# One layer of a hybrid encoder: TensorE's instructions kept in the order of the kernel's text, the other engines ordered by a timeline model

## The chip, the cores and the metric

The kernel runs on one NeuronCore of a Trainium2 chip. The core has five engines with an instruction stream each: TensorE (PE in the profile, its weight loads PEld), VectorE (DVE), ScalarE (ACT), GpSimd (POOL) and SyncE (SP, whose stream issues most of the DMAs; SPq is its queue). Each engine works through its own stream in order; an instruction that needs another engine's result waits at its place, and what stands behind it in the same stream waits too. The metric is the time of one execution on the device in microseconds (us), lower is better.

## The reference

A sequence of 2048 positions of width 1024, in float32, goes through one layer. Cut to what matters:

```python
h = rmsnorm(x, norm_mix_w)
proj = h @ w_in                       # 1024 -> 5648 columns
u_b, u_c, u_h, z, xbc, dt_raw = split(proj)
y_a = u_b * conv3(u_c * u_h)          # short gated convolution
xs, B, C = split(silu(conv4(xbc)))
dt = softplus(dt_raw + dt_bias)       # 16 heads
y_b = ssd_scan(xs, dt, -exp(a_log), B, C) + d_skip * xs
y_b = grouped_rmsnorm(y_b * silu(z))
x = x + concat(y_a, y_b) @ w_out
h = rmsnorm(x, norm_mlp_w)
x = x + square(relu(h @ w_up)) @ w_down   # 1024 -> 4096 -> 1024
return rmsnorm(x, final_norm_w)
```

The scan is chunked: inside a chunk the running sum of `dt * a` gives decay factors exp(difference of two running sums); between chunks a state per head is carried on.

## The kernel before

**The products.** Positions lie in four blocks of 512 (two make a half), features on the 128 partitions. A float32 operand is split in two: a part rounded to fp32r by ScalarE (`whi` L100 for weights, `uh` L205 or L347 for activations), and the rest, by a subtraction on VectorE (`wlo` L101, `ul` L206 or L348). A float32 product is then three fp32r matmuls with 128x128 weights and 512 columns: high by high, high by low, low by high (L113 to L115, L276 to L278). The large projections combine their blocks into seven products in place of eight (the names b11, t1, t2, b21, t3, b22, t4 stand for them), so VectorE also makes sums of weights and activations, and adds products (L730, L874, L1018) when it takes them out of PSUM.

**The stages**, in the order of the text of `trunk`: `start` (RMSNorm of the first two blocks: square and sum into `facc` L489/L492, the column sums `pst` L132, the root `rs` L144, its spread over partitions `prb` L178, the scaling L501; then the gate's first columns and the part for dt); `first_half` (the in-projection of half 0, with VectorE and ScalarE normalising half 1 beside it, L371 to L380); `second_half` (of half 1, with the scan of half 0 beside it); the out-projection with the scan of half 1 beside it; the MLP up and down; the last RMSNorm.

**The dt part** (`dt_part`, L616 to L676), once for each of the four blocks: a sum of products `pd` on TensorE (L625), a copy by ScalarE (L629), four small transposes `pt` on TensorE (L633), the softplus as a chain of small VectorE operations on 128x64 (L635 to L656, with one Exp on ScalarE, L644, in it), the running sums `pc` on TensorE (L662, L663), a copy (L664), a transpose `pr` on TensorE (L671), and the stores to `dt_d` and `rd_d` from which the scan loads. It is a generator, and its caller draws it on between pieces of other work:

```python
nc.vector.tensor_tensor(                                  # L656, end of the softplus
    out=three(e), in0=three(v), in1=self.a_neg..., op=ALU.mult)
yield
yield
pc = psum("tp", "pc", 2)
nc.tensor.matmul(pc[:, 0:64], tri, e, start=True, stop=True)   # L662
```

and in `start`, for each of the two first blocks, after the block's z columns (`group`, L534):

```python
for _ in dts:
    next(work, None)      # work: normalising, or sums of activations; no matmuls
```

**The scan** (`Scan`, L1181) handles 32 pieces (a chunk of one of two head groups), half of them beside `second_half` and half beside the out-projection. A piece has its loads (`load`, L1205: `xd` L1220, `bc`, `dec`, all from DRAM, on SP's queue), a front (L1245: transposes `ptx` L1253 and `ptb` L1255 and the product L1256 on TensorE; then on ScalarE the copies `xtok` and `btok`, eight Relu activations `dec` L1267 and one Exp L1268) and a back (L1278: `yo` L1287, `st` L1289, `yd` L1292 on TensorE, the state's update L1302/L1303 on VectorE, the norm's `pss` L1317). Both are generators; `after` in `second_half` and `hook` in `unit` (L1464) draw one step between products, so the text itself lays the scan's small matmuls between the large ones.

**What sets the order.** All of `trunk` is written inside a tile context. The program's text gives each engine a list of instructions in text order; when the context closes, a scheduler sets the order in which each engine's stream holds them, by a model of how long each takes and what it waits for. Dependencies become semaphore waits. In the kernel before this is done with the context's defaults for all engines, with no order written out by hand: TensorE's stream departs from the text at 47 places (an instruction that stands behind one with a later place in the text), 809 of its 11,514 instructions stand somewhere else than in the text, by up to 95 places forwards and 48 back. The dt part's small matmuls and the scan's transposes are among them.

## Time and profile before

| | us |
|---|---|
| median of 3 timed runs | 2664.36 (2661.9 to 2666.43) |
| the profiled execution | 2658.11 |
| its span in the trace | 2656.4 |
| TensorE busy | 2602.2 (98%), 12,024 matmuls |
| VectorE busy | 1874.3 (71%) |
| ScalarE busy | 1436.5 (54%) |
| GpSimd busy | 146.1 (6%) |
| DMA | 536.96 MB, the one queue q1 60.9% of 16 engines' span |
| mean granted TensorE clock | 0.995 |

The span runs from the first to the last record of the trace; the profiled execution's own time is 1.7 us longer, and 6.25 us under the median of the timed runs. A group's row reads: line, engine, operation, output tile and input tiles, shapes, count; then the busy time of all of them, the mean of one, and the idle time just before them with what ended most of it. A row of the timeline reads: start, duration, engine, line, operation, and in square brackets the engine's idle time before it and whose work released it.

### The profile page before, as it was taken

The numbers are of one execution on the slowest core, as the hardware profiler recorded it, in microseconds if no ns is written. First come the engines' busy times: TensorE is split into PE (matmuls) and PEld (weight loads), VectorE is DVE, ScalarE is ACT, GpSimd is POOL, SyncE is SP. The second block draws the span as 40 slices with busy tenths as digits, with TensorE's granted clock in tenths as the row PEclk, the third lists the DMA queues.
The fourth block names the chain that finished last, engine by engine and source line by source line (L and its number), as shares of the span: only waits on it lengthen the run. The fifth ranks groups of instructions, "written<-read, shape, count | busy, mean of one in ns | idle before, by whom it ended". The sixth has DMA issues, their size and how long they took to land.

```text
span 2656.4 us, 33528 instructions
## 1 busy us (share of the span) xinstructions
PE 2602.2 (98%) x12024; PEld 2124.8 (80%) x12024; DVE 1874.3 (71%) x2524; ACT 1436.5 (54%) x2178; POOL 146.1 (6%) x162
## 2 busy tenths in 40 slices
PE   7999999999999999998999999999999999999998
PEld 5788888778877888776888888888887888888887
DVE  7977867667667666666678675744447877888985
ACT  6654345766567566857336555755555434444443
POOL 0010000111111001111000000000000000000001
PEclk9999999999999999999999999999999999999999
DMA  3545735555555578867566786765558554665762
GB/s 145 196 174 182 278 143 202 182 152 174 169 161 168 165 262 267 254 200 232 193 208 214 258 315 254 258 234 178 209 183 297 155 152 153 206 219 165 249 209 71
DMA packets 292871, 536.96 MB, mean 202 GB/s; under 512 B 26208, under 2 KB 141920, under 8 KB 292704
## 3 DMA queue, kind: packets, MB, share of 16 engines
q1 hardware_dynamic: 292704, 534.82, 60.9%
q8 instruction: 94, 1.54, 0.2%
q14 instruction: 73, 0.60, 0.1%
HBM read 354.89 MB, written 179.83 MB: 201 GB/s over the span
## 4 chain that ended last, share of the span: by engine, by line
PE 59%; issue 26%; ACT 5%; DMA 4%; DVE 4%; POOL 1%; SPq 0%; POOLq 0%; DVEq 0%; ACTq 0%
PE px L276 9%; PE px L277 9%; PE px L278 9%; PE py L276 4%; PE py L277 4%; PE py L278 4%; PE pm L113 4%; PE pm L114 4%; PE pm L115 3%; PE pw L276 2%; PE pw L277 2%; PE pw L278 2%; ACT whi L100 1%; ACT dec L1267 1%; DMA dec<-rd_d 1%
## 5 line engine op out<-in xcount | busy, mean ns | idle before, releaser
L276 PE MATMUL px<-uh,whi 128*128 128x512 f32 x1672 | 657.7, 393 | 6.8 <-DVE acc L1018 1.8
L278 PE MATMUL px<-uh,wlo 128*128 128x512 f32 x1672 | 652.2, 390 | 0.0
L277 PE MATMUL px<-ul,whi 128*128 128x512 f32 x1672 | 651.9, 390 | 0.0
L276 PEld LDWEIGHTS px<-uh,whi 128*128 128x128 f32 x1672 | 314.5, 188 | 82.2 <-DVE acc L1018 3.2
L101 DVE TENSOR_TENSOR wlo<-wraw,whi 128x1024 fp32r<-128x1024 f32 x214 | 223.2, 1043 | 222.2 <-ACT whi L100 216.4
L278 PEld LDWEIGHTS px<-uh,wlo 128*128 128x128 f32 x1672 | 314.4, 188 | 66.4 <-issue 0.2
L277 PEld LDWEIGHTS px<-ul,whi 128*128 128x128 f32 x1672 | 314.6, 188 | 63.5
L100 ACT CAST whi<-wraw 128x1024 fp32r<-128x1024 f32 x214 | 193.6, 905 | 302.5 <-PE px L277 223.4
L276 PE MATMUL py<-uh,whi 128*128 128x512 f32 x836 | 327.4, 392 | 4.4 <-DVE acc L1018 3.4
L100 ACT CAST whi<-s 128x1024 fp32r<-128x1024 f32 x210 | 219.7, 1046 | 206.8 <-PE py L277 81.8
L277 PE MATMUL py<-ul,whi 128*128 128x512 f32 x836 | 325.6, 389 | 0.0
L278 PE MATMUL py<-uh,wlo 128*128 128x512 f32 x836 | 325.4, 389 | 0.0
L101 DVE TENSOR_TENSOR wlo<-s,whi 128x1024 fp32r<-128x1024 f32 x210 | 255.2, 1216 | 79.9 <-ACT whi L100 78.1
L113 PE MATMUL pm<-uh,whi 128*128 128x512 f32 (+1 forms) x648 | 253.1, 392 | 2.1 <-ACT uh L205 2.1
L114 PE MATMUL pm<-ul,whi 128*128 128x512 f32 (+1 forms) x648 | 249.9, 386 | 0.0
L115 PE MATMUL pm<-uh,wlo 128*128 128x512 f32 (+1 forms) x648 | 249.5, 385 | 0.0
L276 PEld LDWEIGHTS py<-uh,whi 128*128 128x128 f32 x836 | 156.9, 188 | 39.8 <-DVE acc L1018 3.8
L278 PEld LDWEIGHTS py<-uh,wlo 128*128 128x128 f32 x836 | 156.9, 188 | 33.0 <-DVE wlo L101 0.2
L277 PEld LDWEIGHTS py<-ul,whi 128*128 128x128 f32 x836 | 157.0, 188 | 32.0
L276 PE MATMUL pw<-uh,whi 128*128 128x512 f32 x418 | 163.5, 391 | 0.7 <-ACT pw L283 0.7
L347 ACT CAST uh<-rh 128x1024 fp32r<-128x1024 f32 (+1 forms) x128 | 120.3, 943 | 80.4 <-PE py L278 62.4
L278 PE MATMUL pw<-uh,wlo 128*128 128x512 f32 x418 | 162.9, 390 | 0.0
(232 smaller groups left out, 3763.2 us busy)
## 6 DMA issues: line engine op xcount, KB each, us to landing
hid_d<-e SPq DMA_DIRECT2D x96, 512.0 KB, 3.9
rh<-hid_d SPq DMA_DIRECT2D x96, 512.0 KB, 4.4
wraw<-w_in SPq DMA_DIRECT2D x68, 512.0 KB, 3.9
wraw<-w_down SPq DMA_DIRECT2D x104, 256.0 KB, 3.7
wraw<-w_up SPq DMA_DIRECT2D x48, 512.0 KB, 4.5
dec<-rd_d SPq DMA_DIRECT2D x32, 512.0 KB, 5.8
wraw<-w_out SPq DMA_DIRECT2D x32, 512.0 KB, 5.1
x_d<-xt SPq DMA_DIRECT2D x64, 256.0 KB, 3.2
```

The lines of the kernel that those rows point to most:

```text
L100: nc.scalar.copy(hi, raw)
L101: eng.tensor_tensor(out=lo, in0=raw, in1=hi.bitcast(F32), op=ALU.subtract)
L113: nc.tensor.matmul(out, whi, hi, start=(k == 0), stop=False)
L114: nc.tensor.matmul(out, whi, lo, start=False, stop=False)
L115: nc.tensor.matmul(out, wlo, hi, start=False, stop=(k == nk - 1))
L276: nc.tensor.matmul(p, hi, h[0], start=not seeded and k == 0, stop=False, **kw)
L277: nc.tensor.matmul(p, hi, h[1], start=False, stop=False, **kw)
L278: nc.tensor.matmul(p, lo, h[0], start=False, stop=(k == len(g) - 1), **kw)
L347: nc.scalar.copy(p[i][0], t)
L1267: nc.scalar.activation(dec[:, i], dec[:, i], AF.Relu, bias=t["a"][:, i : i + 1], scale=-1.0)
```

## The change

Two arguments of the tile context. The first has the scheduler use its timeline model of the engines and queues in place of the simpler one. The second puts the whole of `trunk` in a scope in which TensorE's instructions aren't moved: its stream is the text's order. The other engines are ordered by the scheduler as before, now with the other model.

```diff
-    with tile.TileContext(nc) as tc:
-        trunk(tc, *args, out)
+    with tile.TileContext(nc, schedule_with_timeline_sim=True) as tc:
+        with tc.manual_schedule(engines={mybir.EngineType.PE}):
+            trunk(tc, *args, out)
```

The instructions and their number stay the same on TensorE, VectorE and SyncE; ScalarE has three loads of its function table fewer. TensorE now departs from the text nowhere. On VectorE 1,397 of some 2,500 instructions stand elsewhere than before (by up to 53 places), on ScalarE 946 of some 2,180 (up to 30), on SyncE 813 of some 1,500 (up to 61). Three places follow; names carry the number of the buffer (it differs from one build to the other), and "x4" is four such rows in a run.

TensorE in `start`, the running sums of block 0's dt part (`pc`, `pr`), before: they stand between matmuls of the z columns (`pm`), 84 instructions further behind the `pt` transposes than in the text.

```order
L113 MATMUL pm<-uh_461,whi 128x512
L114 MATMUL pm<-ul_462,whi 128x512
L115 MATMUL pm<-uh_461,wlo 128x512
L113 MATMUL pm<-uh_469,whi 128x512
L662 MATMUL pc<-dts,tri 128x64
L663 MATMUL pc<-dts,ones_r 128x64
L114 MATMUL pm<-ul_470,whi 128x512
L115 MATMUL pm<-uh_469,wlo 128x512
L113 MATMUL pm<-uh_477,whi 128x512
L671 MATMUL pr<-ident,dts 64x128
L625 MATMUL pd<-uh_409,wdt 32x512
```

The same place now:

```order
L625 MATMUL pd<-uh_296,wdt 32x512
L625 MATMUL pd<-ul_297,wdt 32x512
L633 MATMUL pt<-ident,dts 128x32 x4
L662 MATMUL pc<-dts,tri 128x64
L663 MATMUL pc<-dts,ones_r 128x64
L671 MATMUL pr<-ident,dts 64x128
L113 MATMUL pm<-uh_411,whi 128x512
L114 MATMUL pm<-ul_412,whi 128x512
```

`pt`, `pc` and `pr` now follow one another, with none of the z columns' matmuls between them: those that stood there are ahead of the `pd` products or behind `pr`. Block 1 and the two blocks of half 1 have the same four groups in the text, in `start` side by side as here.

VectorE over the same stretch, the end of block 0's softplus and what follows it, before:

```order
L653 SCALAR_TENSOR_TENSOR dts<-dts 128x64
L206 TENSOR_TENSOR ul_290<-x_183,uh_289 128x512
L655 SCALAR_TENSOR_TENSOR dts<-dts 128x64
L520 TENSOR_TENSOR x_183<-x_218,x_183 128x512
L656 TENSOR_TENSOR dts<-dts,hb 128x64
L206 TENSOR_TENSOR ul_462<-x_216,uh_461 128x512
L664 COPY dts<-pc 128x128
L206 TENSOR_TENSOR ul_470<-x_216,uh_469 128x512
L666 TENSOR_TENSOR dts<-dts 128x64
L672 COPY dts<-pr 64x128
```

and now:

```order
L377 TENSOR_TENSOR facc<-lx 128x512
L650 TENSOR_SCALAR dts<-dts 128x64
L652 SCALAR_TENSOR_TENSOR dts<-dts 128x64 x6
L380 TENSOR_TENSOR facc<-facc,lx 128x512
L652 SCALAR_TENSOR_TENSOR dts<-dts 128x64
L380 TENSOR_TENSOR facc<-facc,lx 128x512
L653 SCALAR_TENSOR_TENSOR dts<-dts 128x64
L655 SCALAR_TENSOR_TENSOR dts<-dts 128x64
L656 TENSOR_TENSOR dts<-dts,hb 128x64
L380 TENSOR_TENSOR facc<-facc,lx 128x512 x2
L664 COPY dts<-pc 128x128
```

The small steps of the softplus stand among the sums of squares of the next half (`facc` from `lx`, a tile loaded from DRAM), in place of the low parts `ul` and the sums of activations.

TensorE in `second_half`, the opening of the scan of half 0 (`ptx`, `ptb`), before:

```order
L276 MATMUL py<-uh_3713,whi 128x512
L277 MATMUL py<-ul_3714,whi 128x512
L278 MATMUL py<-uh_3713,wlo 128x512
L276 MATMUL py<-uh_3717,whi 128x512
L1287 MATMUL yo<-bc,state_3777 128x128 x3
L1253 MATMUL ptx<-ident,xd 128x128 x4
L1255 MATMUL ptb<-ident,bc 128x128
L1256 MATMUL ptb<-bc 128x128
L1287 MATMUL yo<-bc,state_3777 128x128
L277 MATMUL py<-ul_3718,whi 128x512
```

and now:

```order
L276 MATMUL py<-uh_3605,whi 128x512
L277 MATMUL py<-ul_3606,whi 128x512
L278 MATMUL py<-uh_3605,wlo 128x512
L1253 MATMUL ptx<-ident,xd 128x128 x4
L1255 MATMUL ptb<-ident,bc 128x128
L1256 MATMUL ptb<-bc 128x128
L276 MATMUL px<-uh_3655,whi 128x512
L277 MATMUL px<-ul_3656,whi 128x512
L278 MATMUL px<-uh_3655,wlo 128x512
```

The transposes stand 43 instructions earlier in the stream, after the product of the step before, where the text draws the scan's first front. (The `yo` products moved behind them, to the text's place.)

## The prediction

> **What bounds the kernel now.** I read the busy shares, then the waits of TensorE, then its busy time by stretches.
>
> ```profile
> PE 2602.2 (98%) x12024; PEld 2124.8 (80%) x12024; DVE 1874.3 (71%) x2524; ACT 1436.5 (54%) x2178; POOL 146.1 (6%) x162
> ...
> PE pst L132 <- DVE facc L492: 12.7, 1, 12.7
> ...
> 0.00:100.00 100.00, 83.66 (x362) 1.00 0.46 165
> 235.00:450.00 215.00, 215.00 (x949) 1.00 0.58 208
> 545.00:970.00 425.00, 422.18 (x2088) 1.00 0.55 171
> ```
>
> (Waits: us in total, times, longest. Stretches: window, length, PE busy and matmuls, clock, DMA share, GB/s.) TensorE is busy for 98% of the span. Its idle time is 2656.4 - 2602.2 = 54 us, of which 16.3 lie in the first 100 us, 12.7 of those at the very first product, before there is anything else to do. In the steady stretch a matmul costs 215/949 = 0.2265 us. So TensorE is the bound, and there are 41 us at most that a better order could win from behind the start's first wait. On the other side every microsecond that TensorE newly waits lengthens the run, since nothing later has slack to give it back.
>
> The method follows from this. TensorE's text order is known. For each place of it I took the time at which TensorE gets there before (that of the matmul standing behind that place) and the time at which the operands are ready before. Where ready is later than arrival, TensorE will now stand; it used to fill this time with matmuls that the text has later. Then I shift by what the other engines' new order puts ahead of the producer. Most of the stream comes out ready in time; the terms below are the places that don't.
>
> A wait also costs clock. After 2.92 us of idling the matmuls start 0.43 us apart:
>
> ```profile
> 1219.30 0.33 PE L1255 MATMUL ptb<-ident,bc 128*128 128x128 f32 x1 [2.92 <-DVE state L1303]
> ...
> 1219.94 0.63 PE L114 MATMUL pm<-ul,whi 128*128 128x512 f32 x1
> 1220.37 0.63 PE L115 MATMUL pm<-uh,wlo 128*128 128x512 f32 x1
> ...
> 1223.33 0.40 PE L113 MATMUL pm<-uh,whi 128*128 128x512 f32 x1
> ```
>
> From 1219.94 to 1223.33 are 8 matmuls: 3.39 us instead of 8 x 0.2265 = 1.8, so 1.6 us on top of a wait of this length.
>
> **Term 1, the first normalisation: +6.** The first low part `ul` (L206) stands ahead of the scalings before; now the order of VectorE puts seven more scalings (L501) and four sums (L489/L492) ahead of it.
>
> ```profile
> 19.96 0.69 DVE L206 TENSOR_TENSOR ul<-x,uh 128x512 fp32r<-128x512 f32 x1
> 20.56 2.07 DVE L501 SCALAR_TENSOR_TENSOR x<-x,cv,facc 128x512 f32<-128x512 f32 x3
> 28.48 1.28 ACT L461 ACT_TABLE_LOAD   x1
> 29.77 0.22 ACT L461 ACTIVATE hb<-hb 128x16 f32<-128x16 f32 x1
> 33.98 3.08 DVE L492 TENSOR_TENSOR facc<-facc,sq 128x512 f32<-128x512 f32 x4
> ```
>
> 7 x 0.69 + 4 x 0.77 = 7.9 us later for the first L114. The Exp of `hb` (L461) with its table load now stands ahead of the root on ScalarE, 1.28 + 0.22 = 1.5 more. The scalings have to be done anyway, and TensorE runs through the rest of the first columns faster once they are; I give back 3.4 and take 6, bounds 0 (all swallowed by the later products) and 9.4. The Trainium skill ("ScalarE: Activation LUTs", What ACT_TABLE_LOAD costs) adds a drain of some 1.38 us to each load, 2.66 in all. In the trace the load at 28.48 lasts 1.28 and the Exp starts at 29.77, right behind it, so the row shows no drain; by the page term 1 would be 1.4 more.
>
> **Term 2, the dt part of blocks 0 and 1: +44.** This is the largest piece. In the text the running sums `pc` stand directly behind `pt` and `pr` directly behind `pc`; the softplus chain on VectorE lies between `pt` and `pc`.
>
> ```profile
> 50.26 0.43 PE L633 MATMUL pt<-ident,dts 32*128 32x32 f32 x4
> 69.79 0.33 PE L662 MATMUL pc<-dts,tri 128*128 128x64 f32 x2
> 70.93 0.27 PE L671 MATMUL pr<-ident,dts 128*64 128x128 f32 x1
> ...
> 75.99 0.43 PE L633 MATMUL pt<-ident,dts 32*128 32x32 f32 x4
> 97.66 0.33 PE L662 MATMUL pc<-dts,tri 128*128 128x64 f32 x2
> ...
> 494.09 0.28 DVE L635 TENSOR_REDUCE dts<-pt 128x64 f32<-128x128 f32 x1
> 503.71 0.41 PE L662 MATMUL pc<-dts,tri 128*128 128x64 f32 x2 [0.57 <-DVE dts L656]
> ```
>
> Before, TensorE did matmuls of the z columns from 50.6 to 69.8; now they stand behind `pr`, or are already done. Block 0: `pc` starts 69.79 - 50.26 = 19.5 after `pt`, `pr` another 1.1 later, 20.6 together. VectorE has 12 operations of 128x512 more ahead of L656 (8.2 us at 0.69), among them the sums from `lx`, which comes by DMA; against that it gets rid of some of the operations that stood between the steps of the chain. I take 26. Block 1: from the end of `pt` (75.99 + 0.4) to 97.66 are 21.3; nothing is added ahead in the new order, and about 5 are saved since VectorE has run ahead during the first wait: 16, with 1.6 for the clock 18. Sum 44. The lower bound is the chain with VectorE free for it, which half 1 shows: 494.09 to 503.71, 9.6 each, 19 for both. The upper one is 20.6 + 8.2 + 21.3 + 1.1 + 2 x 1.6 and 3 for a late `lx` (a load of `xd` takes 3.1 to land, below), 57.
>
> **Term 3, the opening of each scan: +18.** `ptx` is now reached where the text has it:
>
> ```profile
> 467.03 0.39 PE L276 MATMUL px<-uh,whi 128*128 128x512 f32 x1
> 472.11 0.33 SPq L309 DMA_DIRECT2D a<-w_in  x1
> 473.91 0.43 SPq L1220 DMA_DIRECT2D xd<-xs_d  x1
> DMA to landing us min/median/max: 3.1/3.1/3.1
> 477.99 0.60 PE L1253 MATMUL ptx<-ident,xd 128*128 128x128 f32 x4
> 480.46 2.45 ACT L1267 ACTIVATE dec<-dec,dd 128x128 f32<-128x128 f32 x8 [0.53 <-DMA bc<-xs_d]
> ...
> 973.99 0.39 PE L113 MATMUL pm<-uh,whi 128*128 128x512 f32 x1
> 976.55 0.43 SPq L1220 DMA_DIRECT2D xd<-xs_d  x1
> 982.23 0.60 PE L1253 MATMUL ptx<-ident,xd 128*128 128x128 f32 x4
> ```
>
> `xd` lands 3.1 us after its issue, at 477.0, 9.9 after TensorE's arrival. SP's queue now has the weight load L309 behind the scan's loads, and this load waited for VectorE until 472.11, so `xd` goes out up to 3 us earlier: 9.9 - 3 + 1.6 = 8.5 (bounds 4 and 11.5). The second scan: 982.23 - 973.99 = 8.2 late, and I find nothing that brings the load forward: 8.2 + 1.6 = 9.8 (bounds 5 and 11).
>
> **Term 4, the dt part of half 1: +16.** Here the text has other matmuls between the groups, so only the rest is exposed (the first `pc` is in term 2's rows).
>
> ```profile
> 499.35 0.39 PE L276 MATMUL pw<-uh,whi 128*128 128x512 f32 x1
> 523.77 0.39 PE L276 MATMUL py<-uh,whi 128*128 128x512 f32 x1
> 533.01 0.41 PE L662 MATMUL pc<-dts,tri 128*128 128x64 f32 x2 [1.60 <-DVE dts L656]
> ```
>
> Arrival 499.35, start 503.71, 0.57 of it idle already: 3.8; the copy of `pd` on ScalarE (L629) now stands behind the eight Relus (2.45 us, term 3's row) and their Exp, which takes about as long, 4.9 against a slack of about 2: 2.9 more, 6.7. The second: 9.2 - 1.6 + 1.6 for the clock = 9.2. Bounds together 8 and 20.
>
> **Term 5, later places: +26.5.**
>
> ```profile
> 226.06 3.35 DVE L172 RECIPROCAL facc<-facc 128x512 f32<-128x512 f32 x1
> ...
> 1235.18 0.39 PE L113 MATMUL pm<-uh,whi 128*128 128x512 f32 x1
> ...
> 1243.42 0.80 PE L1317 MATMUL pss<-ssq,ones_r 128*128 128x128 f32 x2 [5.37 <-DVE facc L1492]
> ...
> 2023.32 0.39 PE L276 MATMUL px<-uh,whi 128*128 128x512 f32 x1
> 2034.05 0.50 PE L276 MATMUL py<-uh,whi 128*128 128x512 f32 x1 [3.38 <-DVE acc L1018]
> 2035.68 0.79 PE L276 MATMUL px<-uh,whi 128*128 128x512 f32 x1 [0.43 <-DVE acc L1018]
> ...
> 2621.44 0.28 PE L113 MATMUL pm<-uh,whi 128*128 128x256 f32 x1
> ```
>
> `pss` at 1235.18: 8.2 late, 5.4 idle already, and a square behind eight Relus: 4. The down projection: the accumulation read at 2035.6 is wanted at 2023.3, 12.3 late, less the 3.8 idle in the rows there, and the product before it is late too, which I count for 2.5: 6. The last norm (from 2621.44): 3. Seven places with 0.4 to 3.8 us late, such as those behind the reciprocal of 3.35 us: 5.5 in all (estimate). The rest of the scan: TensorE isn't moved, but ScalarE's order puts the next piece's Relus, which wait for a load, ahead of copies that TensorE waits for: +8, taken near the lower end of -10 to +45 (no row before shows it; the stretch from 545 to 970 had only 2.8 us of idling, and each of 32 pieces would lose at most the Relus' 2.45 less what lies open).
>
> **The sum:** 6 + 44 + 18 + 16 + 26.5 = 110.5. On the profiled execution's 2658.1 this is 2768.6; the median of the runs shown lies 6.25 above that execution, so 2775.
>
> **Rivals.** *Chains alone:* the timeline model brings the producers forward where it sees TensorE stand. For it: VectorE is busy for 71% only, SP's load moved aside. Against: in the new order VectorE's big operations stand among the small ones of block 0. Term 2 falls to 19, term 3 to 9, term 4 to 8: 42 less, 2733. *Relus first:* ScalarE's order costs each of 32 scan pieces 1.4 us more than the 8 of term 5: +45, 2820. For it: the order of ScalarE does put them first; against: ScalarE is 54% busy and the pieces are some 13 us apart ((970 - 545)/32). *The other side:* in text order TensorE loses only the two chains of 9.5 us, or even less if the model puts them ahead of everything, while the timeline order removes the stalls that stand now: at most the 41 us found above, since the first 12.7 remain. If it removed all and lost 22 it would be 2645; it decides if terms 2 to 4 stay under the waits won. The rows of term 2 speak against it: nothing stands between `pt`, `pc` and `pr`. *It does nothing:* only 47 departures in 11,514 instructions; but the dt part is among them.
>
> **How the numbers follow.** Forecast (2775) 0.60, chains alone (2733) 0.17, Relus first (2820) 0.17, the other side (2645) 0.04, nothing (within 0.2% of 2664, about what a measurement here can tell) 0.02. The terms' bounds make 2775 uncertain by about 30 either way (they don't all go to one end); reaching down past 2733 and up past 2820 leaves about 2 in 10: 2720 to 2826. Slower 0.60 + 0.17 + 0.17 = 0.94, same 0.02, faster 0.04.
>
> **What would show it.** Right: TensorE's waits list `pc` L662 for VectorE's L656 with over 10 us each in the first 130 us, `ptx` for the load of `xd` at both openings with 5 to 9, and its busy time is near 2602 plus some 10 for slow clock; and it is busy for some 35 to 45 of the first 100 us, not 83.66. Wrong: `pc` waits of 9 or less (term 2 is the chain alone); idling spread over the scan's stretches (545 to 970 and 1000 to 1234) of more than 10 us (Relus first); or a wait at `pc` that is hidden, with the stalls listed at the top gone (the other side).

## The result and the profile after

The changed kernel takes 2855.8 us (median of 4 runs, 2846.9 to 2862.8) where the kernel before takes 2664.0 beside it: a ratio of 1.072 (95% interval 1.069 to 1.075), 192 us more. The prediction said slower, 2775 us, 2720 to 2826. The direction was right, the size was not: 110 us had been forecast, and the time lies above the range.

The page of the changed kernel, span and busy shares:

```profile
span 2850.8 us, 33696 instructions
...
PE 2643.6 (93%) x12024; PEld 2148.9 (75%) x12024; DVE 1884.2 (66%) x2524; ACT 1434.3 (50%) x2175; POOL 146.8 (5%) x162
```

TensorE does the same 12,024 matmuls. Its busy time rose by 41 us (2602.2 to 2643.6: most of it matmuls that ran at the slow clock behind waits, see the last section), its idle time from 54 to 207 us. What TensorE waited for (operation, for whom, us in total, times, longest), the largest entries:

```profile
PE pc L662 <- DVE dts L656: 52.0, 4, 21.5
PE px L276 <- DVE acc L1018: 26.4, 10, 15.2
PE ptx L1253 <- DMA xd<-xs_d: 14.7, 2, 7.8
PE px L276 <- ACT s L727: 12.9, 4, 6.9
PE st L1289 <- ACT whi L100: 12.6, 5, 4.5
PE pst L132 <- DVE facc L492: 12.5, 1, 12.5
PE pss L1317 <- DVE facc L1492: 11.6, 2, 10.3
PE yd L1292 <- DVE dec L1275: 7.2, 8, 1.9
```

The first, second, third and seventh rows are places that the prediction names (of the second, 15.2 us at the place named, the rest spread over the down projection); the sixth is the start's first product, which waited as long before. The fourth, fifth and eighth are not: they lie in the two scan stretches, and there TensorE waits for ScalarE or for the decay factors. Of ScalarE's own waits one grew fivefold. Before, the list of what L1267 waits for has 21.3 us for `dec`, in 13 pieces:

```profile
  DMA dec<-rd_d: 21.3, 13
```

and after, in the view of ScalarE's waits:

```profile
ACT dec L1267 <- DMA dec<-rd_d: 112.5, 28, 11.3
```

**Where the time went, by stage.** All kernels of this case do the same matmuls, so I cut each run at the same counts of matmuls started (266, 1949, 2313, 4428, 4492, 5784, 5811, 9185, 9327, 11598, out of 12,024) and took each piece's length less that of the kernel before, in us. At a cut, a few matmuls may stand in the other piece, so a unit or two here or there means nothing; and each column is one execution, where the executions of the changed kernel spread over 16 us in all. The prediction gave its 8 us for the scans and its 5.5 us for seven places without a stage; the column "predicted" shares them out by hand. "Text only", "model only" and so on are the experiments below.

| stage (us from the start in the kernel before) | predicted | the change | text only | model only | change, Relus held | text only, start respread |
|---|---|---|---|---|---|---|
| start (13 to 79) | 50 | 50.3 | 37.0 | 15.5 | 48.2 | 8.5 |
| first half (79 to 462) | some 2 | 11.7 | 5.3 | 35.5 | 11.7 | 4.8 |
| scan 1 opens, dt of half 1 (462 to 541) | 24.5 | 27.2 | 16.3 | 2.5 | 24.0 | 19.6 |
| scan 1 (541 to 972) | about half of 8 | 21.8 | -1.6 | 39.4 | 15.1 | -0.5 |
| scan 2 opens (972 to 985) | 9.8 | 6.9 | 7.4 | 2.1 | 8.5 | 8.8 |
| scan 2 (985 to 1235) | about half of 8 | 33.2 | 3.2 | 27.9 | 5.6 | 2.0 |
| `pss` at its end (1235 to 1247) | 4 | 4.6 | 3.3 | -7.1 | -5.0 | 3.1 |
| rest of the out-projection, MLP up (1247 to 2007) | some 2 | 7.8 | 1.2 | 37.5 | 8.4 | 2.8 |
| down begins (2007 to 2048) | 6 | 12.4 | 5.9 | 6.8 | 12.2 | 6.9 |
| down (2048 to 2566) | some 1.5 | 16.2 | 5.8 | 21.1 | 15.4 | 3.2 |
| tail (2566 to 2648) | 3 | 3.0 | 2.9 | -1.8 | 1.4 | 3.5 |
| all | 110.5 | 195.3 | 86.8 | 179.2 | 145.5 | 62.7 |

In the start, the openings, `pss` and the tail the terms hold. 47 of the missing 85 us are in the two scan stretches (55 measured, 8 forecast), 30 in the stretches that I had down for a few us in all (first half, MLP, down), 6 at the beginning of the down projection.

**How an early Relu costs.** This is ScalarE in the changed kernel, in the first scan, around TensorE's longest wait for a copy `s` (start, duration, engine, line, operation, idle before it and its releaser):

```profile
827.19 2.16 ACT L1267 ACTIVATE dec<-dec,dd 128x128 f32<-128x128 f32 x7 [3.16 <-DMA dec<-rd_d]
829.37 1.28 ACT L688 ACT_TABLE_LOAD   x1
830.66 1.06 ACT L688 ACTIVATE cacc<-cacc 128x1024 f32<-128x1024 f32 x1
831.63 0.38 ACT L1267 ACTIVATE dec<-dec,dd 128x128 f32<-128x128 f32 x1
831.92 0.56 ACT L727 COPY s<-py 128x512 f32<-128x512 f32 x1
832.50 1.28 ACT L1268 ACT_TABLE_LOAD   x1
833.80 1.06 ACT L1268 ACTIVATE dec<-dec 128x1024 f32<-128x1024 f32 x1
834.76 0.61 ACT L1311 ACTIVATE stmp<-y 128x512 f32<-128x512 f32 x1
835.39 1.28 ACT L688 ACT_TABLE_LOAD   x1
836.68 1.06 ACT L688 ACTIVATE cacc<-cacc 128x1024 f32<-128x1024 f32 x1
837.65 1.03 ACT L100 CAST whi<-wraw 128x1024 fp32r<-128x1024 f32 x1
838.58 0.58 ACT L727 COPY s<-px 128x512 f32<-128x512 f32 x1
```

and TensorE at its end:

```profile
839.21 0.79 PE L276 MATMUL px<-uh,whi 128*128 128x512 f32 x1 [6.86 <-ACT s L727]
```

ScalarE stands for 3.16 us, because the next thing in its stream is a Relu whose load has not landed. Behind the Relus come two Silus, the Exp, three loads of the function table and, last, the copy that frees the PSUM bank for TensorE's next product. TensorE stands for 6.86 us. The load is only a part of this: without the 3.16 us the copy would still come some 3.7 us late (an estimate, 6.86 - 3.16), for the work that the order puts ahead of it.

In the second scan the chain is another. ScalarE's copy `xtok` stands behind the Relus, VectorE makes `stmp` from it, and TensorE's product `st` needs `stmp`:

```profile
1237.96 2.45 ACT L1267 ACTIVATE dec<-dec,dd 128x128 f32<-128x128 f32 x8 [3.94 <-DMA dec<-rd_d]
...
1244.70 0.56 ACT L1258 COPY xtok<-ptx 128x512 f32<-128x512 f32 x1
1245.29 1.29 DVE L1273 TENSOR_TENSOR stmp<-xtok,dd 128x512 f32<-128x512 f32 x2 [3.28 <-ACT xtok L1258]
1246.73 2.05 PE L1289 MATMUL st<-stmp,btok 128*128 128x512 f32 x2 [4.13 <-DVE stmp L1273]
```

This scan has six waits of more than half a microsecond at `st`, 16.7 us together, and before each of them ScalarE had stood at the Relus for 3.9 to 11.3 us. (The list above puts most of them down to `whi` L100. That cast ended last, but `st` doesn't read it.) The loads are not the cause: `dec` is issued 14.5 us (median) ahead of the `st` of the piece before, 11.9 in the kernel before, and takes 6.3 us to land in both.

In the order of the streams, loads of the function table left out, the first of a piece's Relus stands 8 to 11 places ahead of the square of the piece before in the first scan (before: from 3 behind to 12 ahead), and 11 to 48 ahead in the second (before: 9 to 33). ScalarE's waits in the second scan, before (985 to 1235 us) and after (1103 to 1386):

```profile
ACT dec L1267 <- DMA dec<-rd_d: 11.8, 6, 4.6
```

```profile
ACT dec L1267 <- DMA dec<-rd_d: 57.5, 11, 11.3
```

### The profile page after: what moved, and what is told of

It reads as the page before. It is cut to its first block, busy times and chain, and to the rows that moved or that the text cites. A ratio compares the mean times of both kernels' runs of the same rounds, so it can differ in the third digit from the quotient of the medians.

```text
span 2850.8 us, 33696 instructions
## 1 busy us (share of the span) xinstructions
PE 2643.6 (93%) x12024; PEld 2148.9 (75%) x12024; DVE 1884.2 (66%) x2524; ACT 1434.3 (50%) x2175; POOL 146.8 (5%) x162
## 4 chain that ended last, share of the span: by engine, by line
PE 53%; issue 25%; DMA 8%; ACT 6%; DVE 6%; SPq 1%; POOL 0%; POOLq 0%; DVEq 0%; ACTq 0%
PE px L276 8%; PE px L278 8%; PE px L277 8%; PE py L276 4%; PE py L277 4%; PE py L278 4%; DMA dec<-rd_d 4%; PE pm L113 3%; PE pm L114 3%; PE pm L115 3%; PE pw L276 2%; PE pw L277 2%; PE pw L278 2%; ACT dec L1267 2%; ACT whi L100 1%
## 5 line engine op out<-in xcount | busy, mean ns | idle before, releaser
L276 PE MATMUL px<-uh,whi 128*128 128x512 f32 x1672 | 664.6, 397 | 56.8 <-DVE acc L1018 26.4
L100 ACT CAST whi<-wraw 128x1024 fp32r<-128x1024 f32 x214 | 193.8, 906 | 330.2 <-PE px L277 261.3
L100 ACT CAST whi<-s 128x1024 fp32r<-128x1024 f32 x210 | 219.6, 1046 | 251.4 <-PE py L277 113.5
L114 PE MATMUL pm<-ul,whi 128*128 128x512 f32 (+1 forms) x648 | 253.6, 391 | 4.2 <-DVE ul L206 4.2
L277 PE MATMUL pw<-ul,whi 128*128 128x512 f32 x418 | 163.4, 391 | 0.0
```

Source lines behind the costliest of these rows:

```text
L100: nc.scalar.copy(hi, raw)
L114: nc.tensor.matmul(out, whi, lo, start=False, stop=False)
L276: nc.tensor.matmul(p, hi, h[0], start=not seeded and k == 0, stop=False, **kw)
L277: nc.tensor.matmul(p, hi, h[1], start=False, stop=False, **kw)
```

## The experiments

Theory from the profile above: two causes. TensorE's text order costs at the places of terms 1 to 5, and the timeline model's order of ScalarE costs in the scans, by itself. Rival: it is all the text order, and ScalarE's waits are what a late TensorE leaves.

**1. Text order alone.** The first argument is taken back:

```diff
-    with tile.TileContext(nc, schedule_with_timeline_sim=True) as tc:
+    with tile.TileContext(nc) as tc:
         with tc.manual_schedule(engines={mybir.EngineType.PE}):
```

> TensorE in the order of the text, the other engines ordered by the simpler model as before. My theory has two causes in the change: the text order of TensorE (the dt part, the openings of the scan, the down projection) and the timeline model's order of ScalarE, which puts the next scan piece's Relus (L1267) ahead of copies, squares and casts and has them wait there for a load. By it this kernel keeps the first and loses the second: 2664 + 51 (start) + 18 (two openings) + 17 (half 1's dt) + 12 (down projection) + some 10 = about 2770, range 2750 to 2790, and ScalarE waits about 21 us for the load of dec, as before. The rival (all of it is TensorE's text order, and the Relus' waits are what a late TensorE leaves) expects 2840 to 2860 and over 100 us of waits for dec.

Measured: 2744.8 us (2742.5 to 2745.9), ratio 1.032 (1.030 to 1.034), a little under the theory's range, far from the rival's. TensorE's waits:

```profile
PE pc L662 <- DVE dts L656: 33.6, 4, 14.5
PE pst L132 <- DVE facc L492: 16.8, 2, 12.8
PE ptx L1253 <- DMA xd<-xs_d: 16.3, 3, 8.3
PE px L276 <- DVE acc L1018: 12.7, 9, 6.8
PE pss L1317 <- DVE facc L1492: 8.6, 1, 8.6
```

But for the start's first product (12.8 of the 16.8 us of `pst`, as long as before), all five are places where the text has a matmul directly behind something that isn't ready, and nothing else is on the list above 5 us. ScalarE's wait for `dec` is 18.8 us, and the scan stretches cost -1.6 and 3.2 us. So 87 of the 195 us are the text order's alone; the other 108 come when the model is added to it.

**2. The model alone.** The second argument is taken back, and TensorE is ordered by the model too.

```diff
     with tile.TileContext(nc, schedule_with_timeline_sim=True) as tc:
-        with tc.manual_schedule(engines={mybir.EngineType.PE}):
-            trunk(tc, *args, out)
+        trunk(tc, *args, out)
```

> The other half alone: all engines, TensorE too, ordered by the timeline model. My theory (ScalarE's order costs by itself): 2700 to 2750, with ScalarE's waits for dec over 80 us, TensorE's idling in the two scan stretches some 40 to 60 us, and no wait over 5 us at pc L662. The rival (text order is the whole cause): within 1% of before, 2640 to 2690.

Measured: 2845.8 us (2837.1 to 2851.1), ratio 1.070 (1.067 to 1.072). Neither had it. The mechanism is there: 111.8 us of waits for `dec`, 39.4 and 27.9 us lost in the scan stretches although TensorE is free to go round. Their idling, 50.8 us, is what the theory expected; the one wait at `pc`, 5.6 us, is a little over its 5. But the model's order of TensorE also loses 35.5 us in the first half and 37.5 in the MLP, where nothing of the scan runs. There the waits are small and many, some with these rows, the first from the first half, the second from the MLP:

```profile
PE px L276 <- ACT whi L100: 7.0, 8, 0.9
...
PE px L276 <- ACT e L877: 9.3, 27, 1.4
```

So the two halves of the change don't add up: 87 for the text, 179 for the model, 195 for both. Holding TensorE to the text takes away what the model would do to TensorE's own order (first half 35.5 to 11.7, MLP 37.5 to 7.8) and puts the text's waits in its place.

**3. ScalarE in text order too.**

```diff
-        with tc.manual_schedule(engines={mybir.EngineType.PE}):
+        with tc.manual_schedule(engines={mybir.EngineType.PE, mybir.EngineType.Activation}):
```

> The change, with ScalarE kept in the text's order as well as TensorE; in it the Relus of the next scan piece stand behind the square of the piece before and behind their own piece's copies. My theory: ScalarE's waits for dec fall from 112 us to under 40 and the two scan stretches give back some 30 to 50 of their 52 us: 2800 to 2825; if ScalarE's text order brings stalls of its own, these show at other lines. The rival: 2845 or more, since TensorE's order is the same.

Measured: 2939.9 us (2936.4 to 2943.1), ratio 1.106 (1.104 to 1.107). The total is where the rival has it, but not for the rival's reason. ScalarE no longer waits for `dec`, and the second scan falls from 33.2 us over before to 6.5, as the theory wants; but the first scan goes to 76.8 and the first half to 81.1, for a reason of their own:

```profile
PE px L276 <- ACT pw L283: 70.0, 15, 12.3
PE py L276 <- ACT buf L774: 48.0, 11, 6.8
```

In the text's order ScalarE's copies out of PSUM stand behind work that waits for VectorE (109.1 us in 24 waits at the Silu `cacc` L688). The total tells nothing about the theory; the second scan does.

**4. The start free.** TensorE held to the text only from the first half on:

```diff
             ws = proj.start()
+            ctx.enter_context(tc.manual_schedule(engines={mybir.EngineType.PE}))
             ws = proj.first_half(ws)
...
-        with tc.manual_schedule(engines={mybir.EngineType.PE}):
-            trunk(tc, *args, out)
+        trunk(tc, *args, out)
```

> The change, with TensorE held to the text only from the first half on; in the start it is ordered by the timeline model, which lays matmuls between pt, pc and pr again. My theory (a wait of TensorE is never given back): the two pc waits of 21.5 and 13 us go, and with them what pr and the slow clock add: 40 us, 2810 to 2822. The rival (later work is bound by VectorE or the loads and would wait that much more): 2840 to 2856.

Measured: 2825.8 us (2824.1 to 2827.8), ratio 1.063 (1.061 to 1.064): 30 us back, not 40. The start falls from 50.3 to 17.7 us over before. The wait at the second `pc` is gone, that at the first falls from 21.5 to 6.1 us, and what is left of the start is about what the model's own order of it costs (15.5 with the model alone). Of the 32.6 us won there 5 are lost in the first half and 4 in the second scan; most of the gain stays to the end.

**5. The Relus held back.** The change, with one edge added that orders ScalarE's stream and adds no wait (the first piece of each scan has none):

```diff
-            nc.scalar.activation(q4, y, AF.Square)
+            self.squared = nc.scalar.activation(q4, y, AF.Square)
...
-                nc.scalar.activation(dec[:, i], dec[:, i], AF.Relu, bias=t["a"][:, i : i + 1], scale=-1.0)
+                relu = nc.scalar.activation(dec[:, i], dec[:, i], AF.Relu, bias=t["a"][:, i : i + 1], scale=-1.0)
+                if n > self.begin:
+                    why = mybir.DependencyInfo(mybir.DependencyClass.NoSync, mybir.DependencyReason.DATA)
+                    tc.add_manual_dep(relu.ins, self.squared.ins.name, why, reason="behind the square")
```

> The change, with one order added on ScalarE: a scan piece's eight Relus (L1267) stay behind the square (L1311) of the piece before, in both scans; no wait, no load and nothing of TensorE's order is touched. My theory now: the timeline model's early Relus make the two scan stretches slow (54 us more than before there; ScalarE waits 45 us for dec in the first scan, 79 in the second). So the wait for dec falls from 112 us to under 25 and 35 to 55 us come back: 2800 to 2822. The rival (the timeline's order of VectorE, or of the queue, holds TensorE up in the scans, and ScalarE only waits along): 2845 or more.

Measured: 2804.0 us (2801.0 to 2805.3), ratio 1.053 (1.051 to 1.055): 52 us back, within the theory's ranges. ScalarE's wait for the load is nearly gone:

```profile
ACT dec L1267 <- DMA dec<-rd_d: 7.9, 7, 2.0
```

By stages the second scan gives back 27.6 us and `pss` behind it 9.6. The first scan gives back only 6.7 of its 21.8. TensorE's order is untouched by the edge, but the scheduler set a few other instructions elsewhere too: in the second scan 66 of VectorE's 249, 27 of ScalarE's 192 others and 40 of 208 DMA issues, by at most 6 places. This is no way back to the order before: VectorE's instructions of this scan still stand elsewhere than before at 179 of 248 places, where the change has 181. So, small shifts aside, it is not VectorE's order that held the second scan up. None of the waits at `st` above is left there; `yd` waits 7.1 us for the decay factors. What is left in the first scan stands mostly in one row of TensorE's waits, for the bank that ScalarE's copy `xtok` frees:

```profile
PE pss L1320 <- ACT xtok L1258: 9.3, 5, 5.3
```

**6. The same edge with the model alone.** The edit of 5 on the kernel of 2.

> The timeline model for all engines, TensorE not held to the text, with the same added order on ScalarE. If the early Relus are the model's doing whatever TensorE's order is, the 42 and 29 us that the scan stretches cost there fall by more than half: 2846 down to 2785 to 2810. If they matter only where TensorE can't go round them: within 10 us of 2846.

Measured: 2780.8 us (2776.3 to 2792.5), ratio 1.046 (1.043 to 1.048): 65 us back, a little more than forecast, though only 36 of them come from the scan stretches. The second scan falls from 27.9 to -2.4, the first only from 39.4 to 34.0, and 24.5 of the gain is in the MLP, where the edge orders nothing and the model came to another order. In the second scan the early Relus cost whatever TensorE's order is; in the first they are the smaller part in both kernels.

**7. The start's text respread.** Text order and the simpler model (the kernel of 1), with `pt`, `pc` and `pr` drawn between pieces of the z columns:

```diff
-                self.group(bb, ws, (0, 1, 2), work)       # block 0
+            dts0, dts1 = self.dt_part(0), self.dt_part(1)
+            self.group(0, ws, (0, 1, 2), work)
...
+            next(dts0)                                     # pd of block 0
+            self.group(0, ws, (3,), drawn(work, {0: (dts0,)}), "mw")     # pt inside
...
+            next(dts1)                                     # pd of block 1
+            self.group(1, ws, (0, 1, 2), drawn(work, {0: (dts1,), 4: (dts0, dts0), 5: (dts0,)}))
...
+            self.group(1, ws, (3,), work, "mw")            # then pc and pr of block 1
```

(Cut; the comments are added here. `drawn` calls the named generators behind the matmuls of the k given.)

> TensorE in text order and the simpler model, as in the run with the text order alone (2745), but with the start's text changed: pt of blocks 0 and 1 is drawn ahead of a group of z columns, pc and pr of block 0 inside block 1's group and those of block 1 behind it, so that matmuls stand between them. The same work. If the start's 38 us over before are the two softplus chains that the old text left uncovered, the two pc waits there (24 us) fall under 5 and the time to 2712 to 2730. If VectorE, which has the normalising to do in the same stretch, bounds the start however the text is laid: 2735 to 2750.

Measured: 2717.2 us (2710.0 to 2721.4), ratio 1.021 (1.018 to 1.023). The start goes from 37.0 us over before to 8.5, and no wait for `pc` is left in the first 100 us (23.6 us with the old text). The two uncovered chains were most of the start's cost (28.5 of 37 us).

**8. The Relus behind their own copies as well.** To the edge of 5 a second one, to the copy `btok`:

```diff
+                    tc.add_manual_dep(relu.ins, t["copied"].ins.name, why, reason="behind the copies")
```

> The change with the Relus behind the square of the piece before, as in the run before (2804), and now also behind their own piece's copies xtok and btok, as the text has them. That run left 15 us over before in the first scan, and there TensorE waited 9.3 us at pss for the copy xtok, which frees the PSUM bank. If the Relus ahead of the copy are the cause, this wait falls under 3 us and the first scan to under 8 us over before: 2788 to 2798. If later Relus only shift the wait to yd (which needs the decay factors): 2800 or more, with yd waits over 15 us.

Measured: 2811.4 us (2804.9 to 2812.9), ratio 1.057 (1.054 to 1.059). The wait that I had blamed falls from 9.3 to 1.1 us, and the first scan still goes up, from 15.1 to 21.9 over before: other waits for ScalarE and VectorE take its place, each small, the largest being:

```profile
PE py L276 <- ACT eb L765: 4.0, 1, 4.0
PE px L276 <- ACT pw L283: 3.9, 2, 2.0
```

`yd` waits 10.0 us in the whole run, not over 15. Neither expectation is met as a whole: of the first the wait fell as it said, but not the time; of the second the time is right, but its sign isn't there. The copy is not the cause of the 15 us of the first scan; which part of the model's order of the other engines is, stays open.

**9. Both repairs.** The change with the edit of 5 and the text of 7.

> The change with both repairs: the Relus behind the square, and the start's text with matmuls between pt, pc and pr. If the causes are separate and add up, the 28 us that the new text of the start won in text order with the simpler model come off 2804: 2772 to 2782. If the timeline model's order of VectorE, with sums of the next half among the softplus steps, keeps the start late, less: 2785 to 2800.

Measured: 2785.1 us (2782.3 to 2789.1), ratio 1.047 (1.045 to 1.050): 19 us under the run of 5, where 28 would be the full sum; this is the lower end of the second expectation. The start falls from 48.2 to 26.8 us over before, against 8.5 with the simpler model. So the respread text helps under the model too, but some 18 us of the start are the model's order of the other engines.

**10. The scans opened later.** Text order and the simpler model, with the first front of each scan drawn 48 matmuls later:

```diff
             self.load_rows(begin)
-            yield
+            for _ in range(5 if self.bufs == 1 else 8):
+                yield
             front = self.front(begin)
```

> TensorE in text order with the simpler model (2745 alone), with the first front of each scan drawn 48 matmuls (10.9 us) later in the text. By term 3 of the prediction each opening waits because its load lands 8 to 10 us after TensorE gets there. Then the two ptx waits (16 us) go nearly to zero and with them some slow clock: 2726 to 2733. If the scan's later steps merely come late by as much and are waited for at the end of the stage: 2738 to 2748.

Measured: 2740.2 us (2738.1 to 2743.8), ratio 1.030 (1.028 to 1.032). The waits for `xd` are gone from TensorE's list; the two openings cost 7.1 and 0.5 us in place of 16.3 and 7.4, and `pss` turns from 3.3 to -6.7. But the first scan goes from -1.6 to 14.4 and the stretch behind the second from 1.2 to 9.7. In the latter the wait shows plainly, the last pieces' `pss`, now in another stage:

```profile
PE pss L1317 <- DVE facc L1493: 8.9, 3, 5.2
```

In the first scan ScalarE's wait for `dec` grew from 3.0 us without the edit to 13.8 (in the whole run from 18.8 to 40.9). So the openings' waits are what term 3 said, and moving the scan as a whole only moves the cost, as the second expectation has it.

**11. A control.** The edge of 5 on the kernel before.

> A control: the kernel before (simpler model, TensorE free) with the same added order, a piece's Relus behind the square of the piece before. There the model had the Relus only about one place ahead of or behind that square in the first scan, 10 to 33 ahead in the second, and ScalarE waited 21 us for dec in all. If the pin wins under the timeline model because that model's Relus come too early, it wins little here: 2650 to 2668, and by no more than the 6 us that TensorE idles in the second scan. If the pin helps whatever the model, by setting ScalarE's order in general: 2645 or less.

Measured: 2663.9 us (2660.0 to 2667.7), ratio 1.0015 (1.0005 to 1.0025). The edge wins nothing where the simpler model sets the order; it loses 7 us in the profiled first scan, although ScalarE's wait for `dec` falls to 1.3 us. What it won in 5 and 6 is the model's early Relus, not a better order as such. None of these kernels is faster than the one before.

## Why the prediction was right or wrong

**What bounds the kernel: right.** TensorE is still the bound, and a wait that it gets stays to the end: run 4 took most of two waits away at the start and kept most of what it won.

**Terms 1 and 2 (start, 6 + 44 = 50): right in sum, with the shares shifted.** 50.3 measured. Term 1 is nearer its upper bound. Its place is the one named: the first `L114` waits for `ul` and starts 7.4 us later (before, then after), and `pt` starts at 59.00, 8.7 later than before, where 6 had been taken.

```profile
21.06 0.63 PE L114 MATMUL pm<-ul,whi 128*128 128x512 f32 x1
```

```profile
16.06 1.28 ACT L144 ACT_TABLE_LOAD   x1
17.36 0.26 ACT L144 ACTIVATE rs<-pst,cv 128x4 f32<-128x4 f32 x1
...
28.43 0.79 PE L114 MATMUL pm<-ul,whi 128*128 128x512 f32 x1 [4.16 <-DVE ul L206]
...
59.00 0.40 PE L633 MATMUL pt<-ident,dts 32*128 32x32 f32 x4 [0.80 <-ACT dts L629]
80.92 0.66 PE L662 MATMUL pc<-dts,tri 128*128 128x64 f32 x2 [21.52 <-DVE dts L656]
83.67 0.42 PE L671 MATMUL pr<-ident,dts 128*64 128x128 f32 x1 [1.66 <-DVE dts L664]
...
125.31 0.69 PE L662 MATMUL pc<-dts,tri 128*128 128x64 f32 x2 [12.96 <-DVE dts L656]
```

The root `rs` follows the table load at once (16.06 + 1.28 = 17.34, then 17.36). The Trainium skill ("ScalarE: Activation LUTs", What ACT_TABLE_LOAD costs) would have a drain of 1.38 us to each load that switches the set of functions; this row has no room for one, so term 1's excess isn't that. In run 1, without the model, the first `L114` is not late (20.8), and yet `pt` starts at 57.97: TensorE waits 4.0 us at the second block's `pst`, which the text has 27 places earlier in its stream. The prediction has no term for this place. Term 2's waits are 21.5 and 13.0, and 1.7 at `pr`: nearer to the full chains with VectorE's other work between than to the bare 9.6 each. Run 7 shows that the place in the text is the cause, runs 1 and 9 that the model's order of the other engines makes some 13 to 18 of the 50.

**Terms 3 and 4 (openings and half 1's dt, 18 + 16): right in sum, term 4 with some luck.** 27.2 + 6.9 = 34.1 measured, 34 forecast. The two `ptx` waits are 14.7 us together (15 without the clock had been forecast). The two waits at half 1's `pc` are 2.9 and 14.6 us, where 6.7 and 9.2 had been taken; with the text order alone they are 1.0 and 9.1. The first was put too high, the model lengthens the second, and the two errors nearly cancel.

**Term 5: `pss` (4, measured 4.6) and the last norm (3, measured 3.0) right in size; the down projection's beginning mis-sized** (6, measured 12.4). At `pss` this is partly luck: with the Relus held it takes 5.0 less than in the kernel before (run 5), so the early Relus alone make 9.6 there. At the beginning of the down projection the text alone costs 5.9, as the term had it; the other 6.5 come with the model. TensorE's wait there and the issue of the accumulators' loads on SP's queue, with the text order alone and then in the changed kernel:

```profile
2099.65 9.99 SPq L978 DMA_DIRECT2D acc<-x_d  x16
...
2106.05 0.79 PE L276 MATMUL px<-uh,whi 128*128 128x512 f32 x1 [6.76 <-DVE acc L1018]
```

```profile
2194.46 0.32 SPq L862 DMA_DIRECT2D hid_d<-t  x1
...
2195.31 9.73 SPq L978 DMA_DIRECT2D acc<-x_d  x12
...
2203.89 0.80 PE L276 MATMUL px<-uh,whi 128*128 128x512 f32 x1 [15.17 <-DVE acc L1018]
```

TensorE gets there at 2099.3 (2106.05 - 6.76) in the one and the loads go out 0.4 us later; in the other it gets there at 2188.7 and they go out 6.6 us later, behind the MLP's last store.

**The step that failed is the last of term 5, "the rest of the scan", with "taken near the lower end of -10 to +45".** It measured 55 where 8 had been taken. The mechanism had been named: the Relus that wait for a load, put ahead of copies that TensorE waits for. The size went wrong by the bound that a piece "would lose at most the Relus' 2.45". What a piece loses is set by how long ScalarE stands at the head of the Relus, up to 11.3 us in one wait, and by what stands between them and the copy; everything behind them in the stream stands too. So ScalarE's spare time, the reason given against the rival "Relus first", doesn't help. Runs 5 and 6 show it for the second scan (27.6 us and 30 us come back). For the first, the early Relus are 7 of 22 us; the rest is some other part of the model's order, which run 8 didn't find.

The rival "Relus first" (+45 more, 0.17) was nearly exact for the scans (8 + 45 = 53), partly by chance: it spread its loss evenly over all 32 pieces, and the held Relus give back 34 us in the two scan stretches, most of it in the second, and 9.6 at `pss`.

**The second failure is the term of "seven places" and its neighbours.** For the first half, the MLP and the down projection I had some 5.5 us, and 35.7 were measured (11.7 + 7.8 + 16.2). The text order alone costs 12.3 there (5.3 + 1.2 + 5.8). The method asked only where TensorE would now reach an operand before it was ready in the old order, and took the new order of VectorE and ScalarE as neutral wherever I hadn't looked. Run 2 shows how far from neutral this model is: 179 us by itself.

**The rivals.** "Chains alone" fell: the producers were not brought forward (`pc` waits 21.5 and 13.0, not 9). "The other side" and "it does nothing" fell with the sign. Of the signs that the prediction named, the waits at `pc` and `ptx` came in the size named. TensorE was busy for 51.6 of the first 100 us (35 to 45 named), its busy time rose by 41 us (some 10 named), and the two scan stretches idled for 44.7 us, where more than 10 was named as the sign of "Relus first".

## What to carry to other kernels

An order is worth what the engine at the bound finds ready. In this kernel, with one engine 98% busy, a text order that puts a product directly behind a chain of small operations cost waits of 21.5 and 13.0 us, and laying other matmuls between them in the text (run 7) took most of the start's cost away. What an instruction that waits for a load costs can't be told from how busy its engine is. Nor is an early place dear by itself: in the second scan the Relus stood 9 to 33 places ahead of the square before too, at 11.8 us of waits, and holding them back won nothing there (run 11); at 11 to 48 places they waited for 57.5 us, and holding them back won 28. So in a new order look first at which instructions now reach the head of their stream before their load has landed, and at the copies behind them. And when a change exchanges the rule by which four engines are ordered, the places that one has checked are a lower bound; run each half alone before adding up.

## What was not expected of the hardware

The waits cost more than their length. TensorE's busy time rose by 41 us for the same matmuls, on 153 us more of idling, with the mean granted clock at 0.97 in place of 0.995. By the trace's clock records TensorE was busy at half the clock for 88.4 us, before for 14.9; half of the difference, some 37 us, is the slow clock's share of the 41. In the second scan of the changed kernel the clock was 0.95:

```profile
1103.00:1386.00 283.00, 257.67 (x1302) 0.95 0.71 211
```

against 0.99 for the same matmuls before:

```profile
985.00:1235.00 250.00, 244.33 (x1297) 0.99 0.84 248
```

13 of the 33 us lost there are longer matmuls (257.7 busy instead of 244.3), 20 are idling. No wait there is longer than 4.5 us. The granted clock fell to a half in five stretches, 30.7 us in all (before in one, 3.4 us): four of them around waits of 2.1 to 4.5 us at `st`, one behind a wait of 1.9 us at `yd`. The other waits, of 1.6 us and less, show none. The forecast had charged 1.6 us of clock at four long waits only.
